# A two-layer gated decoder trunk: one ordering edge ahead of the values' block product, and the last 128 tokens sent in quarters

## The chip, the cores and the metric

The kernel runs on one core of a Trainium2 chip. The metric is the device time of one execution in microseconds (us), the median of several runs. The core has five engines, each with its own in-order queue of instructions: TensorE (PE in the profile; its weight loads are listed apart as PEld), VectorE (DVE), ScalarE (ACT), GpSimd (POOL) and SyncE (SP). In this kernel SP's queue issues most loads and stores, POOL's issues the accumulating DMAs, and ACT's queue issues a few stores. Tiles live in the on-chip memories SBUF and PSUM; matmuls write PSUM banks of 128 x 512 float32.

## What is computed

Two layers, each with sliding-window attention and a retention branch merged by sigmoid gates, and a squared-ReLU MLP; 512 tokens, model width 1024. Cut to what matters here:

```python
def hybrid_layer(x, g_mix, w_in, sinks, w_a, w_b, w_out, g_mlp, w_up, w_down):
    h = rmsnorm(x, g_mix)
    z = h @ w_in
    aq, ak, av, rq, rk, rv, rg, ga, gb = jnp.split(z, SPLIT_POINTS, axis=-1)
    ya = sliding_window_sink_attention(rope(aq), rope(ak), av, sinks) @ w_a
    r = chunkwise_retention(rotate(rq), rotate(rk), rv)
    r = r * lax.rsqrt(jnp.mean(r * r, axis=-1, keepdims=True) + EPS)
    r = r.reshape(B, S, RET_V) * jax.nn.silu(rg)
    yb = r @ w_b
    x = x + (jax.nn.sigmoid(ga) * ya + jax.nn.sigmoid(gb) * yb) @ w_out
    x = x + jnp.square(jax.nn.relu(rmsnorm(x, g_mlp) @ w_up)) @ w_down
    return x

def reference(x, ...):
    for l in range(2):
        x = hybrid_layer(x, ...)
    return rmsnorm(x, g_final)
```

The change touches two places: the projections `rg` (the retention's output gates, here their upper 512 columns) and `rv` (the retention's values), which both multiply the normalized input by columns of `w_in`, and the final RMSNorm with the store of the output.

## The kernel before

**Precision and weights.** All products are in float32r and split in two: each operand is written as a high part (`hi`) plus a low part (`lo`), and a product is three matmuls, hi by hi, hi by lo and lo by hi (lines 394, 395 and 396 in the helper `products`; `multiply` in `last_gates` does the same at its own line 1015). Weights come in units of 128 x 1024. A call of `unit()` (line 354) takes the next unit in a fixed order, and before that splits units ahead of it: the load into `raw` is issued on SP's queue, ACT copies `raw` into `hi` (line 342), and DVE subtracts to get `lo` (line 343). There are four buffers each of `hi` and `lo` (`SPLIT + 1`), so a split can start only when a unit that was used earlier has been read by its last matmul.

**Block products.** Several projections are computed by seven products of half-size blocks instead of eight, with sums and differences of blocks formed first. For the moving or stationary side these sums are built by the class `Turned` (`turned[1]` to `turned[4]`); the matching sums of weights are made in memory by accumulating DMAs of POOL and by DVE adds at line 322. Two functions that follow each other in the program use them:

- `last_gates(turned)` (lines 1004 to 1058) has seven products of 24 matmuls of 256 columns each, on three PSUM banks `a`, `b` and `c`. In the program's order they are: quarter (0,0) into `a`; a copy of `a` into `b`; `turned[1]` into `c`; `five = keep(c, -1)`, an ACT copy out of `c` (line 1026); `turned[2]` onto `b`; `sum_two = keep(b, 1)`; quarter (1,0) onto `a`; `put(0, 0)`; quarter (1,1) onto `c`; `put(0, 1)`; `turned[3]` onto `b`; `put(1, 1, b, -1, five)`, which begins with a DVE instruction that reads `b` (line 1033); `turned[4]` onto `b`; `put(1, 0)`. A product that adds onto a bank cannot start before the copy or `put` that reads the bank's earlier state. `done(i)` applies the SiLU (ACT sigmoid at 1062, DVE product at 1063).
- `values(turned)` (lines 925 to 984) has the same seven steps with two weight units each, on two banks at a time, matmuls of 512 columns. Its first product is `multiply(a, quarter(0, 0))` at line 967: 24 matmuls, which need only the normalized input `xh`, `xl` and the first two units of `rv`.

**What sets the order.** The program is written in one stream, and the framework's planner puts each engine's instructions into the order in which it expects them to become ready, program order deciding among ready ones. So instructions of `values` may come ahead of instructions of `last_gates` in TensorE's queue. `tc.issue_after(ins)` puts every instruction that its block traces on the engine of `ins` behind `ins` in that engine's queue. It orders the queue and adds no wait for the result; instructions of other engines in the block are not touched. `latest[0]` is a list cell in which helpers leave the last matmul that they traced.

**The end.** In the last layer the output of each block of 128 tokens is held as two halves of 512 columns: `v`, columns 512 to 1023, and `self.y[0, j, m]`, columns 0 to 511. `Ending.put` (lines 1713 to 1741) adds the last product to `v` (DVE, line 1711), takes the sum of squares (ACT, line 1727, with DVE at 1733), the square root (ACT, line 1735) and the reciprocal (DVE, line 1736). Then DVE scales `v` by that factor and the gain (line 1737) and SP's queue sends it (line 1738), while ACT scales the other half, which already has its gain (line 1740), and ACT's queue sends that (line 1741). The last block is (j, m) = (1, 1). `TOKENS` (line 999) is the pair of slices 0 to 255 and 256 to 511.

Of the kernel before, what the change touches and what calls it, by code (L numbers as in the profile page):

```python
# [12 lines left out]
AF = mybir.ActivationFunctionType  # L13
ALU = mybir.AluOpType
# [4 lines left out]
T = 512  # L19
# [97 lines left out]
def decoder(ctx, tc, xT, x_first, w_in, w_rg, w_rv, w_a, w_b, w_wo, w_up, w_pair, w_down, w_end, tables, decay, band, g_last, out):  # L117
    nc = tc.nc
# [279 lines left out]
    latest, behind, spread = [None], [], []  # L398
# [222 lines left out]
    def layer_body(layer):  # L621
# [299 lines left out]
        def quarter(half, tokens):  # L921
            at = slice(tokens * H, tokens * H + H)
            return [(xh[:, k, at], xl[:, k, at]) for k in range(4 * half, 4 * half + 4)]

        def values(turned):

            a, c = ([bank(ps_mm, "rv") for _ in range(2)] for _ in range(2))
            b = [bank(pool, "rv") for pool in (ps_mm, ps_aux)]
            nc.tensor.matmul(b[1], ones, xh[:, 0, :], start=True, stop=True)
            plus, minus = rms_mix.columns, small.tile([P, NB], F32, tag="ncol", name="ncol", bufs=1)  # L930
            nc.vector.tensor_scalar(minus, plus, -1.0, None, ALU.mult)

            def multiply(ps, moving, start=True):
                for u in range(2):
                    hi, lo = unit("rv", layer)
                    for m in range(2):
                        at = slice(m * P, (m + 1) * P)
                        pairs = []
                        for k in range(2):
                            xh_, xl_ = moving[2 * u + k]  # L940
                            cols = slice(k * T, (k + 1) * T)
                            pairs.append(((xh_[:, at], xl_[:, at]), (hi[:, cols], lo[:, cols])))
                        products(ps[m], pairs, start and u == 0, u == 1, not start)

            def scale(j, m, sign):
                return (plus if sign > 0 else minus)[:, 2 * j + m : 2 * j + m + 1]

            def keep(j, ps, sign):
                got = []
                for m in range(2):  # L950
                    t = temp("kept")
                    nc.scalar.activation(t, ps[m], AF.Copy, scale=scale(j, m, sign))
                    got.append(t)
                return got

            def put(i, j, ps, sign, kept=None):
                for m in range(2):
                    hi, lo = slots.one(), slots.one()
                    if kept:
                        nc.vector.scalar_tensor_tensor(kept[m], ps[m], scale(j, m, sign), kept[m], ALU.mult, ALU.add)  # L960
                        split(view(hi), view(lo), kept[m])
                    else:
                        split(view(hi), view(lo), ps[m], scale(j, m, sign))
                    rv[i, 2 * j + m] = (hi, lo)
                    pace(f32(view(hi)))

            multiply(a, quarter(0, 0))
            for m in range(2):
                nc.scalar.activation(b[m], a[m], AF.Copy)
            multiply(c, turned[1])  # L970
            five = keep(1, c, -1)
            multiply(b, turned[2], False)
            turned.free(0)
            two = keep(1, b, 1)
            multiply(a, quarter(1, 0), False)
            quiet[0] = False
            put(0, 0, a, 1)
            multiply(c, quarter(1, 1), False)
            put(0, 1, c, 1, two)
            multiply(b, turned[3], False)  # L980
            put(1, 1, b, -1, five)
            multiply(b, turned[4], False)
            turned.free(1)
            put(1, 0, b, -1)
# [14 lines left out]
        TOKENS = (slice(0, H), slice(H, T))  # L999
# [4 lines left out]
        def last_gates(turned):  # L1004

            a, b, c = (bank(ps_mm, "rg") for _ in range(3))
            two = [big("z") for _ in range(2)]

            def multiply(ps, moving, start=True):
                hi, lo = unit("rg", layer)  # L1010
                for k, (vh, vl) in enumerate(moving):
                    for n in range(2):
                        o, cols = ps[:, n * H : (n + 1) * H], slice((2 * k + n) * P, (2 * k + n + 1) * P)
                        for w, v in ((hi, vh), (hi, vl), (lo, vh)):
                            nc.tensor.matmul(  # L1015
                                o,
                                w[:, cols],
                                v,
                                start=start and k == 0 and n == 0 and w is hi and v is vh,
                                stop=k == 3 and n == 1 and w is lo,  # L1020
                                skip_group_check=True,
                            )

            def keep(ps, sign):
                t = temp("kept")
                nc.scalar.activation(t, ps, AF.Copy, scale=float(sign))
                return both(t)

            def put(i, j, ps, sign, kept=None):
                v = two[i][:, :, TOKENS[j]]  # L1030
                by = rstd()[:, TOKENS[j]].unsqueeze(1).broadcast_to([P, 2, H])
                if kept is not None:
                    nc.vector.scalar_tensor_tensor(kept, both(ps), float(sign), kept, ALU.mult, ALU.add)
                    nc.vector.tensor_tensor(v, kept, by, ALU.mult)
                else:
                    nc.vector.scalar_tensor_tensor(v, both(ps), float(sign), by, ALU.mult, ALU.mult)

            def done(i):
                for m in range(2):
                    rg[4 + 2 * i + m] = two[i][:, m, :]  # L1040
                    silu(4 + 2 * i + m)

            multiply(a, quarter(0, 0))
            nc.scalar.activation(b, a, AF.Copy)
            multiply(c, turned[1])
            five = keep(c, -1)
            multiply(b, turned[2], False)
            sum_two = keep(b, 1)
            multiply(a, quarter(1, 0), False)
            put(0, 0, a, 1)  # L1050
            multiply(c, quarter(1, 1), False)
            put(0, 1, c, 1, sum_two)
            done(0)
            multiply(b, turned[3], False)
            put(1, 1, b, -1, five)
            multiply(b, turned[4], False)
            put(1, 0, b, -1)
            done(1)
# [622 lines left out]
        class Ending:  # L1681
# [31 lines left out]
            def put(self, i, j, m, ps, sign, at=slice(0, T)):  # L1713
                block = 2 * j + m
                scale = (factor if sign > 0 else negative)[:, block : block + 1]
                if i and not last:
                    if (j, m) == (0, 1):
                        self.add(i, j, m, ps, scale)
                    else:
                        self.join(i, j, m, ps, scale)  # L1720
                    return
                with tc.issue_after(self.queued) if i else ExitStack():
                    self.add(i, j, m, ps, scale, at)
                if last:
                    v = self.y[i, j, m]
                    first, total, both = (sq[:, n * NB + block : n * NB + block + 1] for n in range(3))
                    nc.scalar.activation(temp("junk")[:, at], v[:, at], AF.Square, accum_out=both if i else first)
                    if not i:
                        nc.vector.tensor_tensor(v, v, last_gain[:, i, :], ALU.mult)
                        self.queued = nc.vector.tensor_scalar(first, first, 1.0 / D, EPS, ALU.mult, ALU.add).ins  # L1730
                        return
                    if at.stop < T:
                        nc.vector.scalar_tensor_tensor(first, both, 1.0 / D, first, ALU.mult, ALU.add)
                        return
                    nc.scalar.activation(total, both, AF.Sqrt, bias=first, scale=1.0 / D)
                    nc.vector.reciprocal(total, total)
                    nc.vector.scalar_tensor_tensor(v, v, total, last_gain[:, 1, :], ALU.mult, ALU.mult)
                    nc.sync.dma_start(out[:, block, T:], v)
                    v = self.y[0, j, m]
                    nc.scalar.activation(v, v, AF.Copy, scale=total)  # L1740
                    nc.scalar.dma_start(out[:, block, :T], v)

            def turn(self, i, j, half, pool):
                ps = bank(pool, "turn")
# [268 lines left out]
```

## Time and profile before

| | before |
|---|---|
| median of 3 runs | 1460.27 us (1459.97 to 1462.33) |
| profiled execution, its time | 1461.38 us |
| profiled execution, its span on the core | 1459.6 us |
| granted TensorE clock, mean over the span | 0.999 |
| instructions | 22457 |

The profile is of one execution. Its span runs from the first to the last instruction on the core. Most views list groups or single instructions as: start (us), duration (us), engine, line, operation, output<-inputs, shape; a number in square brackets is the time for which the engine stood idle just before, and what ended it. A view of waits lists who waited for whom, with the total in us, the number of times and the longest. In the views by stretches of time, each row has the stretch, its length, the busy time of PE, PEld, DVE, ACT and POOL with the number of instructions, the granted clock, the mean busy share of the 16 DMA engines and their GB/s. Matmuls are pipelined, so recorded durations overlap, and the distance from start to start is the pace.

### The profile page before, as it was taken

How to read it: one execution, taken by the hardware profiler on the slowest of the kernel's cores; microseconds unless marked ns; L12 is line 12 of the kernel's file. 1: busy time of each engine (PE TensorE's matmuls, PEld its weight loads, DVE VectorE, ACT ScalarE, POOL GpSimd, SP SyncE). 2: the span in 40 equal slices, each digit the busy share in tenths (PEclk: the TensorE clock that was granted, in tenths of full speed). 3: DMA queues.
4: the chain of work that ended last, by engine and by line, in shares of the span. 5: the costliest groups of instructions: out<-in, count | busy, mean ns of one | idle time of the engine just before them, and what ended most of it. 6: DMA issues, size and time to landing. Idle time of an engine off the chain costs nothing.

```text
span 1459.6 us, 22457 instructions
## 1 busy us (share of the span) xinstructions
PE 1447.5 (99%) x8185; PEld 1269.5 (87%) x8185; DVE 1183.1 (81%) x1776; ACT 976.5 (67%) x1593; POOL 222.1 (15%) x335
## 2 busy tenths in 40 slices
PE   9999999999999999999999999999999999999998
PEld 7888888888989999999888888888889899999997
DVE  6977987877898888888778789878688888888885
ACT  6656665543688777777756576655447887777775
POOL 0021002221101111112201110021210011111120
PEclk9999999999999999999999999999999999999999
DMA  7598349999735777666955974499965477777764
GB/s 259 178 292 221 118 134 302 286 275 283 212 115 200 196 190 194 174 178 182 305 174 185 287 201 155 147 314 283 274 185 170 144 196 201 196 189 200 177 188 143
DMA packets 97294, 302.83 MB, mean 207 GB/s; under 512 B 11424, under 2 KB 11552, under 8 KB 90784
## 3 DMA queue, kind: packets, MB, share of 16 engines
q0 software_dynamic: 36512, 129.78, 38.0%
q1 hardware_dynamic: 59952, 170.32, 33.9%
q8 instruction: 64, 1.05, 0.3%
q10 hardware_dynamic: 720, 1.31, 0.2%
q14 instruction: 46, 0.38, 0.1%
HBM read 261.78 MB, written 120.06 MB: 262 GB/s over the span
## 4 chain that ended last, share of the span: by engine, by line
PE 95%; DVE 2%; ACT 1%; issue 0%; DMA 0%; DVEq 0%
PE mm L394 22%; PE mm L396 22%; PE mm L395 22%; PE wo L1354 5%; PE b L394 3%; PE b L395 3%; PE b L396 3%; PE rg L1015 2%; PE rv L394 2%; PE rv L395 2%; PE rv L396 2%; PE mm L410 2%; PE score L780 1%; PE pT L745 1%; PE r L395 1%; PE r L396 1%
## 5 line engine op out<-in xcount | busy, mean ns | idle before, releaser
L342 ACT ACTIVATE hi<-raw 128x1024 fp32r<-128x1024 f32 (+1 forms) x393 | 400.1, 1022 | 264.6 <-PE mm L395 118.4
L343 DVE TENSOR_TENSOR lo<-raw,hi 128x1024 fp32r<-128x1024 f32 (+1 forms) x394 | 459.3, 1175 | 103.1 <-ACT hi L342 101.5
L395 PE MATMUL mm<-xl,hi 128*128 128x512 f32 (+1 forms) x912 | 319.4, 353 | 0.0
L394 PE MATMUL mm<-xh,hi 128*128 128x512 f32 (+1 forms) x912 | 318.5, 353 | 0.7 <-ACT xh L420 0.7
L396 PE MATMUL mm<-xh,lo 128*128 128x512 f32 (+1 forms) x912 | 315.6, 352 | 0.0
L394 PEld LDWEIGHTS mm<-xh,hi 128*128 128x128 f32 x912 | 173.1, 190 | 23.3 <-ACT xh L420 1.4
L395 PEld LDWEIGHTS mm<-xl,hi 128*128 128x128 f32 x912 | 173.3, 190 | 21.9
L396 PEld LDWEIGHTS mm<-xh,lo 128*128 128x128 f32 x912 | 171.9, 190 | 21.4
L395 PE MATMUL mm<-r,hi 128*128 128x256 f32 (+1 forms) x608 | 189.2, 311 | 0.0
L396 PE MATMUL mm<-r,lo 128*128 128x256 f32 (+1 forms) x608 | 189.0, 311 | 0.0
L394 PE MATMUL mm<-r,hi 128*128 128x256 f32 (+1 forms) x608 | 186.9, 311 | 0.5 <-ACT mm L1529 0.5
L394 PEld LDWEIGHTS mm<-r,hi 128*128 128x128 f32 x608 | 115.7, 190 | 9.1 <-ACT mm L1529 0.7
L395 PEld LDWEIGHTS mm<-r,hi 128*128 128x128 f32 x608 | 115.7, 190 | 8.5 <-DVE r L418 0.4
L396 PEld LDWEIGHTS mm<-r,lo 128*128 128x128 f32 x608 | 115.8, 190 | 6.3
L1679 POOL DMA_DIRECT2D y<-eu x56 | 63.2, 1407 | 368.0 <-DVE eu L1662 367.6
L395 PE MATMUL mm<-lo,r 128*128 128x512 f32 (+1 forms) x276 | 104.4, 388 | 0.0
L396 PE MATMUL mm<-hi,r 128*128 128x512 f32 (+1 forms) x276 | 101.2, 387 | 0.2 <-DVE r L418 0.2
L394 PE MATMUL mm<-hi,r 128*128 128x512 f32 (+1 forms) x276 | 98.2, 389 | 0.3 <-ACT r L417 0.2
L394 PE MATMUL b<-hi,r 128*128 128x512 f32 x180 | 70.5, 391 | 0.0
L395 PE MATMUL b<-lo,r 128*128 128x512 f32 x180 | 70.2, 390 | 0.0
L1354 PE MATMUL wo<-r,hi 128*128 128x256 f32 x384 | 69.3, 283 | 0.0
L283 DVE TENSOR_TENSOR raw<-raw 128x512 f32<-128x512 f32 x56 | 38.5, 688 | 36.0 <-DMA raw<-w_pair_in 31.1
(337 smaller groups left out, 2865.5 us busy)
## 6 DMA issues: line engine op xcount, KB each, us to landing
raw<-w_in_in SPq DMA_DIRECT2D x65, 512.0 KB, 5.6
sums_down<-w_down_in POOLq DMA_DIRECT2D x30, 1024.0 KB, 12.2
sums_up<-w_pair_in POOLq DMA_DIRECT2D x56, 512.0 KB, 11.1
raw<-w_down_in SPq DMA_DIRECT2D x45, 512.0 KB, 7.2
raw<-w_pair_in SPq DMA_DIRECT2D x84, 256.0 KB, 3.6
y<-y POOLq DMA_DIRECT2D x62, 256.0 KB, 9.7
y<-eu POOLq DMA_DIRECT2D x61, 256.0 KB, 8.6
raw<-sums_down SPq DMA_DIRECT2D x30, 512.0 KB, 7.6
```

The lines of the kernel that those rows point to most:

```text
L283: nc.vector.tensor_tensor(raws[i][:, at], last[:, LEFT], last[:, RIGHT], ALU.add)
L342: state["high"] = nc.scalar.activation(hi[:, at], raw[:, at], AF.Copy).ins
L343: nc.vector.tensor_tensor(lo[:, at], raw[:, at], f32(hi[:, at]), ALU.subtract)
L394: nc.tensor.matmul(ps, ah, bh, start=start and i == 0, stop=False, **more)
L395: nc.tensor.matmul(ps, ah, bl, start=False, stop=False, **more)
L396: latest[0] = nc.tensor.matmul(ps, al, bh, start=False, stop=stop and i == n - 1, **more).ins
L410: latest[0] = nc.tensor.matmul(ps, w[:, cols(j, c)], moving[k][low], start=first, stop=bool(final)).ins
L745: nc.tensor.transpose(pt[:, i * P : (i + 1) * P], sm[:, at : at + P], ident)
L780: nc.tensor.matmul(ps[:, g * w : (g + 1) * w], q_s[g][:, c, at], part[:, keys], start=i == 0, stop=i == 1)
L1015: nc.tensor.matmul(o, w[:, cols], v, start=start and k == 0 and n == 0 and w is hi and v is vh, stop=k == 3 and n == 1 and w is lo, skip_g ...
L1354: latest[0] = nc.tensor.matmul(o, w[:, cols], v, start=start and first and n % 2 == 0 and w is hi and v is vh, stop=final and w is lo, ski ...
L1679: nc.gpsimd.dma_start(y[:, 2 * j + m, i * T : (i + 1) * T], t, **how)
```

## The change

Two edits. In `values`, the first product is traced inside `issue_after(latest[0])`, and `last_gates` now leaves its matmuls in `latest[0]`; so each of the first product's 24 matmuls stands behind the last traced matmul of `last_gates` in TensorE's queue, in both layers. At the end, for the block (1, 1) alone, the two scalings and the two stores of 512 columns become four of 256 columns each; of the four stores SP's queue issues three and ACT's queue the last. For the other three blocks the same instructions remain.

```diff
@@ values
-            multiply(a, quarter(0, 0))
+            with tc.issue_after(latest[0]):
+                multiply(a, quarter(0, 0))
@@ last_gates, multiply
-                            nc.tensor.matmul(
+                            latest[0] = nc.tensor.matmul(
                                 o,
                                 w[:, cols],
                                 v,
...
                                 skip_group_check=True,
-                            )
+                            ).ins
@@ Ending.put
-                    nc.vector.scalar_tensor_tensor(v, v, total, last_gain[:, 1, :], ALU.mult, ALU.mult)
-                    nc.sync.dma_start(out[:, block, T:], v)
-                    v = self.y[0, j, m]
-                    nc.scalar.activation(v, v, AF.Copy, scale=total)
-                    nc.scalar.dma_start(out[:, block, :T], v)
+                    w = self.y[0, j, m]
+                    final = (j, m) == (1, 1)
+                    for n, p in enumerate(TOKENS if final else (slice(0, T),)):
+                        nc.vector.scalar_tensor_tensor(v[:, p], v[:, p], total, last_gain[:, 1, p], ALU.mult, ALU.mult)
+                        nc.sync.dma_start(out[:, block, T + p.start : T + p.stop], v[:, p])
+                        nc.scalar.activation(w[:, p], w[:, p], AF.Copy, scale=total)
+                        queue = nc.sync if final and n == 0 else nc.scalar
+                        queue.dma_start(out[:, block, p], w[:, p])
```

## The prediction

> **What bounds the kernel now.** I read the page's engine line first, then what TensorE itself waited for, then the order in which TensorE, ScalarE (ACT) and VectorE (DVE) ran the last gates' block, then the last five microseconds.
>
> ```profile
> PE 1447.5 (99%) x8185; PEld 1269.5 (87%) x8185; DVE 1183.1 (81%) x1776; ACT 976.5 (67%) x1593; POOL 222.1 (15%) x335
> ...
> PE 95%; DVE 2%; ACT 1%; issue 0%; DMA 0%; DVEq 0%
> ```
>
> TensorE is busy for 1447.5 of 1459.6 us and carries 95% of the chain that ended last. So time can be had in two places only: where TensorE stands still between its first and last matmul, and behind its last matmul. Everything else is covered by matmuls.
>
> ```profile
> PE rv L394 <- ACT hi L342: 2.1, 2, 1.0
> PE warm L374 <- DVE ones L369: 1.1, 1, 1.1
> PE mm L394 <- ACT xh L420: 0.7, 1, 0.7
> ```
>
> The longest entry of TensorE's waits is the one this change goes for: twice, once in each layer, a first matmul of the values' block (rv) waits 1.03 us for its high weights. The rest are small and elsewhere.
>
> **The place, as TensorE ran it in layer 0.**
>
> ```profile
> 184.28 0.28 PE L1015 MATMUL rg<-r,lo 128*128 128x256 f32 x1
> 185.59 0.73 PE L394 MATMUL rv<-hi,xh 128*128 128x512 f32 x2 [1.03 <-ACT hi L342]
> 186.16 0.30 PE L1015 MATMUL rg<-xh,hi 128*128 128x256 f32 x1
> ...
> 191.81 0.28 PE L1015 MATMUL rg<-r,lo 128*128 128x256 f32 x1
> 191.93 0.40 PE L395 MATMUL rv<-lo,xh 128*128 128x512 f32 x1
> 192.16 0.40 PE L396 MATMUL rv<-hi,xl 128*128 128x512 f32 x1
> ...
> 196.71 0.39 PE L396 MATMUL rv<-hi,xl 128*128 128x512 f32 x1
> 196.94 0.40 PE L1015 MATMUL rg<-r,hi 128*128 128x256 f32 x2
> ...
> 199.69 0.28 PE L1015 MATMUL rg<-r,lo 128*128 128x256 f32 x1
> 199.81 0.40 PE L394 MATMUL rv<-hi,r 128*128 128x512 f32 x1
> ```
>
> The gates' block has seven products of 24 matmuls. By 184.40 four are done (both that move `turned[1]` and `turned[2]`, and quarters (0,0) and (1,0)). The fifth, quarter (1,1) into bank `c`, starts at 186.16; the sixth, `turned[3]` into bank `b`, ends at 191.93; the seventh, `turned[4]`, again into `b`, runs from 196.94 to 199.81. The values' first product, also 24 matmuls, lies in two holes: 2 of it before the fifth product and 22 between sixth and seventh. Its pace is 0.23 us a matmul (191.93 to 192.16), that of the gates 0.12 (199.69 to 199.81).
>
> The question is what fills these holes once the values' product may not.
>
> ```profile
> 184.48 1.06 ACT L342 ACTIVATE hi<-raw 128x1024 fp32r<-128x1024 f32 x1 [0.26 <-PE rg L1015]
> 185.44 1.07 ACT L1026 ACTIVATE kept<-rg 128x512 f32<-128x512 f32 x2
> ```
> ```profile
> 186.07 0.19 PEld L1015 LDWEIGHTS rg<-xh,hi 128*128 128x128 f32 x1 [0.19 <-ACT kept L1026]
> ```
>
> The fifth product adds onto bank `c`, and `five = keep(c, -1)` must have read `c` first. ACT took the values' weight split first (184.48, when a weight buffer came free, just before the last of the four products ended at 184.28 + 0.28 = 184.56) and the two `keep` copies behind it, from 185.44. The first of the two ends near 186.02, and the weight load of the fifth product is recorded as waiting for just that, until 186.07. So the two rv matmuls did not hold the fifth product up; they used 0.45 us of a hole that ACT makes.
>
> ```profile
> 189.31 0.69 DVE L1033 SCALAR_TENSOR_TENSOR kept<-rg,kept 128x512 f32<-128x512 f32 x1 [2.05 <-PE rg L1015]
> 190.04 0.69 DVE L1034 TENSOR_TENSOR z<-kept,rstd 128x512 f32<-128x512 f32 x1
> 190.65 1.22 DVE L343 TENSOR_TENSOR lo<-raw,hi 128x1024 fp32r<-128x1024 f32 x1
> 191.79 0.68 DVE L1063 TENSOR_TENSOR z<-z,sig 128x512 f32<-128x512 f32 x1
> 192.39 0.68 DVE L1033 SCALAR_TENSOR_TENSOR kept<-rg,kept 128x512 f32<-128x512 f32 x1
> ```
>
> The seventh product adds onto `b` after the sixth, and `put(1, 1, b, -1, five)` (L1033, the second of these) must have read `b` in between: 192.39 to 193.07. Today 22 rv matmuls cover that wait.
>
> **The first edit, part by part.** It adds no instruction and removes none. It adds an ordering edge on TensorE alone, from each of the 24 matmuls to the last gates' matmul, in each layer. The weight splits (ACT, DVE) and loads (SP's queue) that the same block issues get no edge, since they are not TensorE's; I take their order from the trace as it is, because ACT's choice at 184.48 and DVE's chain from 189.31 hang on gates' matmuls that come before any moved one.
>
> First hole: today 184.28 + 0.12 = 184.40 to 186.16 is 1.76 us with 2 x 0.23 us of work, 1.31 lost (the matmuls' own rows). Afterwards the load still begins at 186.07 and the product at 186.16, with nothing in the hole: 1.67 to 1.76 lost. Second hole: today nothing lost. Afterwards L1033 ends at 193.07, a release takes about 0.05 (split ends 185.54, rv's matmul 185.59), and the matmul stands up to 0.09 behind its load (186.07 to 186.16): the seventh product starts at 193.12 to 193.21 where its slot was 191.93, so 1.19 to 1.28 lost. Together 2.86 to 3.04 against 1.31: 1.55 to 1.73 more per layer.
>
> The same places in layer 1:
>
> ```profile
> 907.04 0.28 PE L1015 MATMUL rg<-r,lo 128*128 128x256 f32 x1
> 908.35 0.73 PE L394 MATMUL rv<-hi,xh 128*128 128x512 f32 x2 [1.03 <-ACT hi L342]
> 908.92 0.30 PE L1015 MATMUL rg<-xh,hi 128*128 128x256 f32 x1
> ...
> 914.68 0.40 PE L395 MATMUL rv<-lo,xh 128*128 128x512 f32 x1
> ```
> ```profile
> 915.15 0.69 DVE L1033 SCALAR_TENSOR_TENSOR kept<-rg,kept 128x512 f32<-128x512 f32 x1
> ```
>
> 907.16 to 908.92 is again 1.76, and 915.84 + 0.05 to 0.14 against 914.68 is 1.21 to 1.30. Both layers: 3.1 to 3.5 us; I take 3.3, nearer the rows as they stand.
>
> The product itself then runs as one piece, 24 x 0.23 = 5.5 us, behind the seventh. I cost its move at nothing: its weights were split long before (184.48, and DVE's at 190.65), and what queues behind it (the values' next products) has weights split at or before it. It holds two of the four weight buffers until about 198.8 and 201.5 (seventh product from 193.2, 2.9 long, then 12 x 0.23 for each unit); the splits that wait for those buffers serve the product after the next, not before 201.5 + 5.5 = 207, and need 1.06 (ACT) and 1.22 (DVE). That slack is the cover; gone, each late split would show about 2.3. Nothing later gives the loss back: TensorE's other waits are 0.7 us and less and hang on its own results, so they move along. Nor does a hole of 1.8 us slow the matmuls behind it: in the end's rows below, the granted clock is still 1.00 in the slice to 1456.60, 3.4 us after TensorE let DVE go at 1453.14.
>
> **The second edit.** Today, the end:
>
> ```profile
> 1453.14 0.48 DVE L1711 SCALAR_TENSOR_TENSOR x<-mm,columns,x 128x256 f32<-128x256 f32 x1 [0.18 <-PE mm L396]
> ...
> 1454.80 0.72 ACT L1740 ACTIVATE x<-x,sq 128x512 f32<-128x512 f32 x1 [0.23 <-DVE sq L1736]
> 1454.80 0.75 DVE L1737 SCALAR_TENSOR_TENSOR x<-x,sq,late 128x512 f32<-128x512 f32 x1
> 1455.55 0.37 ACTq L1741 DMA_DIRECT2D y_out<-x  x1
> 1455.58 0.33 SPq L1738 DMA_DIRECT2D y_out<-x  x1
> ```
> ```profile
> 1456.40:1456.60 0.20, 0.00 (x0) 0.00 (x0) 0.00 (x0) 0.00 (x0) 0.00 (x0) 1.00 0.99 379
> ...
> 1457.60:1457.80 0.20, 0.00 (x0) 0.00 (x0) 0.00 (x0) 0.00 (x0) 0.00 (x0) 0.50 0.87 308
> 1457.80:1458.00 0.20, 0.00 (x0) 0.00 (x0) 0.00 (x0) 0.00 (x0) 0.00 (x0) 0.50 0.08 21
> ```
>
> Issue at 1455.55, first bytes at 1456.40 (0.85 later), then 1.4 us of a full stream. A 256-wide DVE instruction takes 0.48 for 0.75 at 512, so the first quarter is ready at 1455.28, 0.27 earlier. Two more DMAs are issued: SP sends at about 1455.30, 1455.64 and 1455.98 (0.33 each), ACT its one near 1455.73. The last first-byte is then due at 1456.83, when half the bytes are still to go, so the stream stays full and ends 0.27 earlier. Unknown is the rate of 1 KB rows. If each took as long as a 2 KB row the stream would double: 1.1 us lost. If size costs nothing: 0.27 won. Only 128 packets of the whole run have between 512 B and 2 KB, by the page; they are the mask's rows of 1 KB, and they ran between 12.05 and 13.5 us:
>
> ```profile
> DMA packets 97294, 302.83 MB, mean 207 GB/s; under 512 B 11424, under 2 KB 11552, under 8 KB 90784
> ```
> ```profile
> DMA packets 320, 0.58 MB, mean 400 GB/s; under 512 B 37, under 2 KB 165, under 8 KB 320
> ```
>
> 400 GB/s with 128 such packets (165 less 37) of 320 in that stretch, where the end's 2 KB rows make 379: nearly no loss. I take 0.25 won.
>
> From issue to landing the list of DMA issues of the last 20 us (median, us) has:
>
> ```profile
> y_out<-x SPq DMA_DIRECT2D x4, 256.0 KB, 2.4
> ```
>
> The Trainium skill ("DMA: Bandwidth & Descriptors", section on the anatomy of one DMA) puts about 2.0 us plus bytes/436e3 on each DMA, so by it the last quarter, issued at 1455.98, would land after 2.3 us, at 1458.28, against 1455.58 + 2.6 = 1458.18 today, and the sum would be 0.35 higher. The trace has 2.4 us for these 256 KB, 0.2 less than the page.
>
> **Sum.** Span 1459.6 + 3.3 - 0.25 = 1462.65. The profiled execution took 1461.38 with 1459.6 of span; the median shown is 1460.27, so the forecast for the median is 1460.27 + 3.05 = **1463.3 us**, own range 1462.9 to 1463.7.
>
> **Rivals.**
> (1) The block runs through: the `keep` and L1033 are arranged so that neither hole stays. For it: both are short, and the 1.03 us wait is what the profile blames. Against: the load at 186.07 waits for `kept`, and no other ready work is recorded between 191.93 and 196.94. Price: 2 x 1.31 + 0.25 won, 1457.4; not slower. It decides if fifth and seventh products start within 0.2 us of their predecessors.
> (2) ACT takes `five` before the values' split: `c` is complete at 184.56, `five` ends 185.2, the fifth product starts near 185.25, 0.91 earlier per layer: 1463.3 - 1.8 = 1461.5. Against: the split was ready first.
> (3) DVE puts one more 1.14 us split ahead of the second L1033, or a split misses its use: 1463.3 + 2.3 = 1465.6. For: DVE is busy without a break from 189.31.
> (4) The order does not change and only the end does: 1460.0. Against: the edge names these very matmuls.
>
> **How the numbers follow.** Forecast 0.66; rivals 0.06, 0.13, 0.09, 0.06. About 0.2% (2.9 us) is what a measurement here can tell from no change, and the forecast lies just above it: of its 0.66 I count 0.43 as slower and 0.23 as within. With (3), slower 0.52; with (2) and (4), within 0.42; faster 0.06, from (1). The range leaves out (1), (3) and half of (4): 1460.0 to 1464.4.
>
> **What would show it.** Right: no rv matmul among L1015's, fifth product still behind `kept`, a new wait of the seventh product's L1015 for DVE L1033 near 1.2 us in both layers, first bytes of the end 0.27 earlier. Wrong: fifth product starting by 185.3, or anything but L1033 ahead of the seventh.

## The result and the profile after

| | before | after |
|---|---|---|
| median, 7 runs each | 1460.27 us (1459.34 to 1462.73) | 1464.68 us (1463.54 to 1467.05) |
| ratio after/before | | 1.0030, 95% interval 1.0019 to 1.0042 |
| span of the profiled execution | 1459.6 us | 1465.3 us (time 1467.05) |
| instructions | 22457 | 22467 |

The change costs 4.4 us. The forecast was 1463.3 with a range to 1464.4: the direction is right, and the median lies 0.28 us beyond the range. In the changed file lines stand one further down in the gates' and values' blocks (1015 is now 1016, 1026 is 1027, 1033 is 1034); the end's scalings are at 1741 and 1743, their stores at 1742 and 1745.

The first three entries of TensorE's waits after the change (who waited for whom, total us, times, longest):

```profile
PE rg L1016 <- ACT kept L1027: 3.0, 2, 1.5
PE rg L1016 <- DVE kept L1034: 2.1, 2, 1.0
PE warm L374 <- DVE ones L369: 1.1, 1, 1.1
```

The old first entry (rv for its `hi`) is gone, and two of the gates' own waits have come in its place, each once per layer. TensorE in layer 0, then in layer 1:

```profile
184.83 0.28 PE L1016 MATMUL rg<-r,lo 128*128 128x256 f32 x1
186.62 0.39 PE L1016 MATMUL rg<-xh,hi 128*128 128x256 f32 x1 [1.52 <-ACT kept L1027]
...
192.35 0.28 PE L1016 MATMUL rg<-r,lo 128*128 128x256 f32 x1
193.68 0.50 PE L1016 MATMUL rg<-r,hi 128*128 128x256 f32 x2 [1.04 <-DVE kept L1034]
...
196.53 0.28 PE L1016 MATMUL rg<-r,lo 128*128 128x256 f32 x1
196.66 0.40 PE L394 MATMUL rv<-hi,xh 128*128 128x512 f32 x1
...
909.58 0.28 PE L1016 MATMUL rg<-r,lo 128*128 128x256 f32 x1
911.38 0.39 PE L1016 MATMUL rg<-xh,hi 128*128 128x256 f32 x1 [1.52 <-ACT kept L1027]
...
917.11 0.28 PE L1016 MATMUL rg<-r,lo 128*128 128x256 f32 x1
918.43 0.50 PE L1016 MATMUL rg<-r,hi 128*128 128x256 f32 x2 [1.04 <-DVE kept L1034]
```

A gates' matmul has a pace of 0.12, so the first hole, layer 0's, is 186.62 - (184.83 + 0.12) = 1.67 us and the second 193.68 - (192.35 + 0.12) = 1.21; layer 1 has 1.68 and 1.20. Before, 1.31 of the first was lost and nothing of the second: 1.57 more per layer. No rv matmul stands among the gates' any more; the first one follows the last gates' matmul at once.

What ACT and DVE ran at these places is what they ran before, in the same order (shifted by 0.55 us):

```profile
185.03 1.06 ACT L342 ACTIVATE hi<-raw 128x1024 fp32r<-128x1024 f32 x1 [0.26 <-PE rg L1016]
185.99 1.07 ACT L1027 ACTIVATE kept<-rg 128x512 f32<-128x512 f32 x2
```
```profile
192.34 0.69 DVE L1064 TENSOR_TENSOR z<-z,sig 128x512 f32<-128x512 f32 x1
192.94 0.69 DVE L1034 SCALAR_TENSOR_TENSOR kept<-rg,kept 128x512 f32<-128x512 f32 x1
```

The end, in order of time, and then the stores' stream (the last two columns are the share of the DMA engines and GB/s):

```profile
1460.19 0.91 ACT L1743 ACTIVATE x<-x,sq 128x256 f32<-128x256 f32 x2 [0.23 <-DVE sq L1737]
1460.19 0.88 DVE L1741 SCALAR_TENSOR_TENSOR x<-x,sq,late 128x256 f32<-128x256 f32 x2
1460.71 0.33 SPq L1742 DMA_DIRECT2D y_out<-x  x1
1461.13 0.37 ACTq L1745 DMA_DIRECT2D y_out<-x  x1
1461.14 0.37 SPq L1745 DMA_DIRECT2D y_out<-x  x1
1461.61 0.45 SPq L1742 DMA_DIRECT2D y_out<-x  x1
```
```profile
1461.50:1461.70 0.20, 0.00 (x0) 0.00 (x0) 0.00 (x0) 0.00 (x0) 0.00 (x0) 0.50 0.67 236
1461.70:1461.90 0.20, 0.00 (x0) 0.00 (x0) 0.00 (x0) 0.00 (x0) 0.00 (x0) 0.50 1.06 338
1461.90:1462.10 0.20, 0.00 (x0) 0.00 (x0) 0.00 (x0) 0.00 (x0) 0.00 (x0) 0.50 0.59 185
1462.10:1462.30 0.20, 0.00 (x0) 0.00 (x0) 0.00 (x0) 0.00 (x0) 0.00 (x0) 0.50 1.00 348
...
1463.10:1463.30 0.20, 0.00 (x0) 0.00 (x0) 0.00 (x0) 0.00 (x0) 0.00 (x0) 0.50 0.51 164
```

Counted from the scalings' start, the first bytes come 0.27 us earlier than before (1461.53 - 1460.19 = 1.34 against 1456.41 - 1454.80 = 1.61, by the packets in the trace). But the stream then has a dip (185 GB/s) and in its full slices runs at 333 to 348 GB/s, where those of the 2 KB rows had 348 to 410, about 380 on average. From first to last byte it takes 1.78 us against 1.51, so its last bytes come 3.1 us behind the scalings' start in both kernels. The span's end comes 5.1 us behind it, against 4.8 before. So the end lost about 0.3 us instead of winning 0.25, and it lost them **behind the last byte**. There SP passes the program's last waits, among them one instruction for each of the eight semaphores that count the transfers of SP's and ACT's queues, before the core may finish. These are SP's instructions from the moment on at which the last store had landed, before and after; the first of each group is the wait that this landing ended:

```profile
L2008 SPq EVENT_SEMAPHORE  x2: 28/28/28, 1458.4 to 1458.4; - x2
```
```profile
L2012 SPq EVENT_SEMAPHORE  x7: 27/28/28, 1463.7 to 1464.1; - x7
```

Two before, seven after, about 0.06 us apart. The semaphore numbers that the trace keeps with each instruction show why: transfers by SP's and ACT's queues are counted by eight semaphores in turn (numbers 100, 102, 104 and 106 to 110, here called 0 to 7), and the last waits ask for them in the order 0 to 7. Before, the last two stores were counted by 6 and 7, the end of that list. Two transfers more move the last four stores to 6, 7, 0 and 1, so the store that lands last is asked for early, and six waits for what has long landed are still to be passed.

### The profile page after: what moved, and what is told of

It reads as the page before. It is cut to its first block, busy times and chain, and to the rows that moved or that the text cites. A ratio compares the mean times of both kernels' runs of the same rounds, so it can differ in the third digit from the quotient of the medians.

```text
span 1465.3 us, 22467 instructions
## 1 busy us (share of the span) xinstructions
PE 1449.1 (99%) x8185; PEld 1270.3 (87%) x8185; DVE 1183.5 (81%) x1777; ACT 976.2 (67%) x1594; POOL 228.0 (16%) x335
```

## The experiments

Each ratio is to runs of the kernel before on the same chip, with its 95% interval. The expectations count a hole from the start of the matmul ahead of it plus 0.23 us, where the sections above and below take 0.12; what they call 1.57 and 1.10 is 1.67 and 1.21 here. Diffs are cut to the lines that matter; `...` marks what is left out.

**The change once more, its two parts alone, and another filling of the first hole.** The change's file unchanged:

> The changed kernel as it is, a second look. Theory: of the 4.4 us, 3.5 are the two new waits of the gates' block (about 1.57 for ACT's kept and 1.1 for DVE's L1034, in each layer, less the 1.2 that before loses there) and 0.3 the end; they must be there again, and the ratio should be near 1.0026 (3.8 us). Rival: the further loss behind 1180 us in the first profile (0.45 + 0.39 us on a weight add whose load landed late) belongs to the change and is there again, and the ratio is 1.003 or more.

1464.05 us against 1460.89, ratio 1.0026 (1.0017 to 1.0035). In its trace the holes are the same to 0.01 us, and the end takes 5.1 us from the scalings' start.

The first edit alone (`edge_only`) and the second alone (`quarters_only`):

```diff
@@ edge_only: values and last_gates as in the change, Ending.put as before
@@ quarters_only: Ending.put as in the change, values and last_gates as before
```

> The first edit alone, the end as before. Theory: +3.5 us (1.0024), with the waits of the gates' block as in the changed kernel and 4.8 us from the reciprocal's last start to the end of the span. Rival (the end is the larger part): below +2 us.

> The second edit alone. Theory: +0.3 us (the 1 KB rows stream at 335 instead of 380 GB/s and the completion comes later, which gives back the 0.25 us by which the first bytes start earlier): span from the last scaling's start to the end 5.1 against 4.8 us; the ratio can't be told from 1. Rival (the prediction's pricing): 0.25 us less than before, 4.55.

The edge alone: 1464.49 against 1460.89, 1.0024 (1.0014 to 1.0034), both holes as in the change, the end 4.8 us. The quarters alone: 1462.19, 1.0008 (0.9999 to 1.0017), the end 5.1 us. The edge carries nearly all of it; the quarters win nothing and probably lose a little. The interval of the quarters alone reaches no change, so that they lose is read from the trace of the end.

`c_first` leaves both edits away and changes the order ahead of the hole: the second half of the third product must wait for the second product, so that bank `c` is done 12 matmuls earlier.

```diff
-            def multiply(ps, moving, start=True):
+            def multiply(ps, moving, start=True, behind=None):
...
+                            with tc.issue_after(behind) if behind is not None and k > 1 else ExitStack():
+                                done_last[0] = nc.tensor.matmul(
...
-            multiply(b, turned[2], False)
+            multiply(b, turned[2], False, done_last[0])
```

> Before, with one other edge: in the gates' block the second half of the turned[2] product stands behind the turned[1] product, so that bank c is complete 1.4 us earlier and its ACT copy runs beside matmuls. No edge on the values' product. Theory (the first hole is ACT's copy out of c, not the values' matmuls at its end): the hole of 1.2 us goes, the fifth product follows at once, and each layer is 0.7 to 1.2 us shorter: -1.4 to -2.4 us, ratio 0.9985 to 0.999. Rival (the hole is set by the weight split of the values): the hole stays and nothing changes.

1460.02 us, 0.9995 (0.9986 to 1.0003), which can't be told from no change. Of the hole 0.24 us is left in layer 0 (183.48 to 183.72), and no wait of a gates' matmul for ACT's `kept` is listed any more. TensorE's waits show where 1.2 us of the gain went:

```profile
PE rg L1018 <- DVE r L418: 1.2, 2, 0.8
```

The second product, taken earlier, now waits for the split of its own operand `r` on DVE, 0.4 us in layer 0 and 0.8 in layer 1.

**The two holes apart, and who makes the first.** In `edge_fifth` the values' first product waits for the fifth gates' product only.

```diff
-            multiply(a, quarter(0, 0))
+            with tc.issue_after(state["fifth"]):
+                multiply(a, quarter(0, 0))
...
```

> Before, with only the end as it was and the values' first product kept behind the fifth gates' product instead of the seventh; it may fill the second hole as before. If the two holes are independent prices: the first hole loses 1.57 instead of 1.31 us per layer, the second stays filled (no wait of the seventh product for DVE's sum), so +0.5 us in all, ratio 1.0003 to 1.0005. If a hole kept filled gives nothing back, because the values' product then ends at another time and what follows it waits: as the whole edge, 1.0024.

1462.53 against 1461.43, 1.0008 (0.9999 to 1.0016). In the trace the first hole is 1.67 us in both layers, and no wait of a gates' matmul for DVE is listed: the second hole is filled again, by rv matmuls. By its holes it costs 2 x (1.67 - 1.31) = 0.7 us, which the interval holds; the whole edge's 1.0024 lies outside it. The holes are separate prices.

In `edge_five` the edge stays, and ACT takes `five` ahead of the values' weight split.

```diff
-                    state["high"] = nc.scalar.activation(hi[:, at], raw[:, at], AF.Copy).ins
+                    with tc.issue_after(state.pop("five")) if name == "rv" and "five" in state else ExitStack():
+                        state["high"] = nc.scalar.activation(hi[:, at], raw[:, at], AF.Copy).ins
...
```

> The edge of the change with the end as before, and ACT takes the first of the two `kept` copies (five) ahead of the values' weight split. Theory: the first hole is made by that split of 1.06 us; it shrinks from 1.57 to between 0.65 and 0.85 us per layer, the second stays at 1.10; 1.5 to 1.8 us less than the edge alone, ratio 1.0012 to 1.0014. Rival: the later split makes DVE's part of it later and with it the second sum, the second hole grows by as much, and the ratio stays at 1.0024.

TensorE in layer 0:

```profile
184.24 0.28 PE L1017 MATMUL rg<-r,lo 128*128 128x256 f32 x1
185.21 0.38 PE L1017 MATMUL rg<-xh,hi 128*128 128x256 f32 x1 [0.69 <-ACT kept L1028]
...
190.93 0.28 PE L1017 MATMUL rg<-r,lo 128*128 128x256 f32 x1
192.19 0.51 PE L1017 MATMUL rg<-r,hi 128*128 128x256 f32 x2 [0.97 <-DVE kept L1037]
```

The first hole is 185.21 - (184.24 + 0.12) = 0.85 instead of 1.67, the second 1.14 instead of 1.21: 0.9 us less per layer. The time is 1462.43 against 1461.43, 1.0009 (1.0000 to 1.0018), where the edge alone had 1.0024. So ACT's order, split first, makes half of the first hole, and the later split harms nothing.

`c3_five` leaves the edge away again and puts both cures together: 6 matmuls held back instead of 12 (`k > 2` in `c_first`'s edit), and `edge_five`'s edit.

> Before without the edge, with two orders changed ahead of the hole: the last 6 matmuls of the third product (turned[2]) are held behind the second's (turned[1]), and ACT takes five ahead of the values' weight split. Theory: of the 1.31 us lost per layer, 0.7 is covered by the 6 matmuls and 0.8 goes with the split, so at most 0.3 is left, 2.0 to 2.6 us less than before, ratio 0.9982 to 0.9987. Rival: as with 12 matmuls held back, part goes into waits for the split of r on DVE, 0.4 us or more per layer, ratio 0.999 and up.

1461.15 against 1461.43, 1.0000 (0.9991 to 1.0009): a miss. ACT shows the reason:

```profile
181.97 1.06 ACT L343 ACTIVATE hi<-raw 128x1024 fp32r<-128x1024 f32 x1 [1.10 <-PE rg L1019]
182.94 0.58 ACT L1030 ACTIVATE kept<-rg 128x512 f32<-128x512 f32 x1
183.41 1.05 ACT L343 ACTIVATE hi<-raw 128x1024 fp32r<-128x1024 f32 x1
```

The values' split does stand behind `five` now, but with `c` done earlier the split before it, of the seventh gates' product's weights, falls just ahead of `five`. TensorE's hole was 183.57 - (182.50 + 0.12) = 0.95 us. `c3_five2` puts `five` ahead of that split too (the edge holds from the second split behind `five` in the program on):

```diff
+                    five, first = state.get("five", (None, len(order)))
+                    with tc.issue_after(five) if i >= first else ExitStack():
...
+                    state["five"] = kept, state["split"] + 1
...
```

> As the kernel before this in the same line (6 matmuls of turned[2] held back, five ahead of the values' weight split), with five also ahead of the weight split one before it, the seventh gates' product's. Theory: in the run before, the hole of 0.85 us per layer was made by that other split, which ACT ran while five was ready; now at most 0.15 us per layer is left of the 1.31, 2.3 to 2.6 us less than before, ratio 0.9982 to 0.9985. Rival: the seventh product's weights come late instead, or the time goes into another wait as with 12 matmuls held back; then 0.999 and up.

ACT, and TensorE at the same place:

```profile
182.02 0.60 ACT L1033 ACTIVATE kept<-rg 128x512 f32<-128x512 f32 x1 [1.22 <-PE rg L1022]
182.51 2.00 ACT L344 ACTIVATE hi<-raw 128x1024 fp32r<-128x1024 f32 x2
```
```profile
182.42 0.28 PE L1022 MATMUL rg<-r,lo 128*128 128x256 f32 x1
182.67 0.39 PE L1022 MATMUL rg<-xh,hi 128*128 128x256 f32 x1
```

The hole is 182.67 - (182.42 + 0.12) = 0.13 us, and no wait of a gates' matmul is left among TensorE's listed waits. The time is 1458.05 us against 1460.68, **0.9984 (0.9975 to 0.9993)**: faster than the kernel before and than the change. The rv matmuls keep the second hole filled, as before the change.

**The end.** Three other forms of the last stores, one profile each:

```diff
@@ tail_rows: before, last block only
+    nc.sync.dma_start(out[:, block, T:].rearrange("p (a t) -> p a t", a=2), v.rearrange("p (a t) -> p a t", a=2))
...
@@ tail_parts: before, last block only, two by SP and two by ACT
+    for q in (slice(0, 64), slice(64, P)):
+        nc.sync.dma_start(out[q, block, T:], v[q])
+        nc.scalar.dma_start(out[q, block, :T], w[q])
@@ tail_22: before, with the change's end but
-    queue = nc.sync if final and n == 0 else nc.scalar
-    queue.dma_start(out[:, block, p], w[:, p])
+    nc.scalar.dma_start(out[:, block, p], w[:, p])
```

> Before, with the last store's two transfers described as 1 KB rows (two per partition) instead of 2 KB; still two transfers, whole scalings. If the row size sets the rate: about 338 GB/s in place of 380, the stream 0.15 to 0.25 us longer, end 4.95 to 5.05 us after the scalings' start. If the number of transfers and their issue set it: 380 GB/s and 4.8 us.

The end came at 4.8 us, but this tested nothing. The packets of that stretch in `tail_rows`, then in the change:

```profile
DMA packets 288, 0.52 MB, mean 262 GB/s; under 512 B 32, under 2 KB 32, under 8 KB 288
```
```profile
DMA packets 576, 0.52 MB, mean 250 GB/s; under 512 B 64, under 2 KB 576, under 8 KB 576
```

The 256 data packets stayed at 2 KB; the change has 512 of 1 KB. So no run sends the end in 1 KB rows without four transfers, and whether the row size or the number of transfers lowers the rate stays open.

> Before, with the last store in four transfers of 64 partitions with 2 KB rows, two by each queue, behind whole scalings. If the row size set the loss: 380 GB/s and an end 4.8 us after the scalings' start, as with two transfers. If the number of transfers set it: 340 GB/s or a later end, 5.0 us and up.

Neither: the end came 6.3 us behind the scalings' start. With 64 partitions a transfer, the stream had half the rate at a full share for its first 1.2 us:

```profile
1457.80:1458.00 0.20, 0.00 (x0) 0.00 (x0) 0.00 (x0) 0.00 (x0) 0.00 (x0) 0.50 1.04 225
...
1459.20:1459.40 0.20, 0.00 (x0) 0.00 (x0) 0.00 (x0) 0.00 (x0) 0.00 (x0) 0.50 1.11 389
```

> The change, but the quarters sent two by SP and two by ACT instead of three and one. If SP's three issues in a row set the end: the last bytes come 0.2 to 0.4 us earlier than with the change, end 4.7 to 4.9 us after the scalings' start. If the rate of 1 KB rows sets it: 335 to 340 GB/s and 5.0 to 5.1 us, as with the change.

The end came at 5.0 us and the stream had 317 to 358 GB/s without a dip, its last bytes 3.0 us behind the scalings' start instead of 3.1: SP's three issues in a row go with the dip, but they are not what sets the end. The last two stores, too, are counted by semaphores 0 and 1, and SP passed seven waits behind the last landing. That raised the theory of the order of waits, which two kernels test. They load decay tables in more pieces, far from the end (`rot_before` one table per layer, two transfers more in all; `rot_quarters` both, six more); the order of all compute engines' instructions is as in `before` and in `quarters_only`, and only the semaphores of the last stores move.

```diff
+            cuts = (0, T // 2, T) if pair == 0 else (0, T)                        # rot_before
+            cuts = (0, T // 4, T // 2, T) if pair == 0 else (0, T // 2, T)        # rot_quarters, with the change's end
-            nc.sync.dma_start(decays[pair], decay[:, 2 * pair : 2 * pair + 2, :])
+            for c0, c1 in zip(cuts, cuts[1:]):
+                nc.sync.dma_start(decays[pair][:, :, c0:c1], decay[:, 2 * pair : 2 * pair + 2, c0:c1])
```

> Before with its end as it was; one decay table per layer is loaded in two pieces, so two transfers more, about a thousand us ahead of the end, and the last two stores are counted by the first two of the eight transfer semaphores instead of the last two. SP's waits behind its last store go through those eight in a fixed order. Theory: the late end of the change is that order: the last store's wait is now followed by 6 waits of 0.06 us instead of 1 or none, and the end comes 5.10 to 5.20 us after the scalings' start instead of 4.81, with the same two transfers of 2 KB rows. Rival: the quarters themselves are what ends late; then 4.8 here.

> Before with the change's end in quarters, and six transfers more in the decay tables' loads, so that the four last stores are counted by the last four of the eight transfer semaphores. Theory (order of SP's last waits): the last store's wait is again the last or last but one, and the end comes 4.70 to 4.80 us after the scalings' start instead of 5.06 to 5.09. Rival (1 KB rows and SP's issues in a row): 5.0 to 5.1 as with the change.

SP's waits behind the last landing, and the scalings' start, in `rot_before` and then in `rot_quarters`:

```profile
L2010 SPq EVENT_SEMAPHORE  x8: 28/28/28, 1459.1 to 1459.5; - x8
...
1455.55 0.75 DVE L1739 SCALAR_TENSOR_TENSOR x<-x,sq,late 128x512 f32<-128x512 f32 x1
```
```profile
L2013 SPq EVENT_SEMAPHORE  x1: 28/28/28, 1458.9 to 1458.9; - x1
...
1455.36 0.88 DVE L1742 SCALAR_TENSOR_TENSOR x<-x,sq,late 128x256 f32<-128x256 f32 x2
```

`rot_before` ends at 1460.7, 5.2 us behind the scalings' start, with the two 2 KB stores of before and without a quarter: the order of waits alone is enough for an end as late as the change's. `rot_quarters` needs a single wait, and SP is through the list 1459.0 - 1455.36 = 3.6 us behind the scalings' start, against 3.7 before and 4.0 in the change. Its span ends at 4.9, not at the 4.7 to 4.8 expected, because the steps of all engines that close the program took 1.3 us behind SP's list here, and 1.1 in the others; one profile doesn't say why.

## Why the prediction was right in direction and short in size

**The bound and the first edit: right.** The fifth product stands behind `kept`, with the load and matmul where the prediction put them: 1.67 us, forecast 1.67 to 1.76. The seventh product's new wait for DVE's second L1033 (now 1034) makes a hole of 1.21 and 1.20 us, forecast 1.19 to 1.28 in layer 0 and 1.21 to 1.30 in layer 1. Per layer the holes are 1.57 longer, forecast 1.55 to 1.73. From the fourth product's last matmul to the values' second product TensorE takes 17.17 us in each layer instead of 15.41: 1.76 more, 3.5 for both, and `edge_only` measures 3.6. So the term of 3.3 was 0.2 too small: the first matmuls behind a hole take about 0.1 us longer than their pace (186.62 to 186.85 is 0.23 instead of 0.12), which the sum left out. `edge_fifth` and `edge_five` show the two holes and their causes one by one.

**The product's move costed at nothing: right.** None of TensorE's waits after the change is for a split that came late behind the moved product, so rival (3) did not occur; `edge_five`, which makes one split later still, bears that cover out.

**The rivals.** (1) fell at once: both holes are there. (2) was wrong for the change, where the split still goes first, but its price was right: `edge_five` forces that order and the fifth product starts 0.82 us earlier per layer, where 0.91 was put down. (4) fell with the order in the trace.

**The second edit: the step that failed.** The prediction said that "the stream stays full and ends 0.27 earlier" and took 0.25 won; measured are about 0.3 lost. Its first part held, the first bytes being 0.27 us earlier. Three things were wrong. The rate of 2 KB rows was carried over: the quarters ran at 333 to 348 GB/s in full slices against about 380. The mask's window, from which the price was taken, holds loads and only 128 such packets. SP's issues were put 0.34 us apart and came 0.43 and 0.47 apart (1460.71, 1461.14, 1461.61), and the stream has a dip behind the first store; the two together eat the 0.27 us (in `tail_22`, which has no dip, the stream lasts 1.68). And the sum ended with the last byte; what SP does behind it was not looked at, though the view of SP's instructions in the trace of before has it. By the end of SP's list the second edit is worth at most 0.1 us won (3.6 us in `rot_quarters`, one profile, against 3.7 before); the order of SP's last waits turned this into about 0.3 lost.

The section of the Trainium skill that the prediction cites ("DMA: Bandwidth & Descriptors", anatomy of one DMA) states its fit, 2.3 us for 128 KB, for DMAs on GpSimd's path; these stores were issued by SP and ACT. The list of DMA issues after the change has 2.1:

```profile
y_out<-x SPq DMA_DIRECT2D x3, 128.0 KB, 2.1
```

So it was luck that the sum by this fit was nearer to the time: the stores did not land later, the last of them 3.5 us behind the scalings' start against 3.6 before.

**The range.** With both terms as measured the sum is 1460.27 + 3.5 + 0.3 = 1464.1, inside the range and at the 1.0026 of the repeat. The remaining 0.6 us of the first measurement lie within its interval. The range was made by which rivals it leaves out and had no room for this scatter, whose size the three runs of before (1459.97 to 1462.33) already showed. The profiled execution after, itself the slowest of its runs, shows two parts of it: 0.55 us are lost within the first 11 us, and a weight load that comes late in layer 1 costs about 1.1. DVE at that load, before and after:

```profile
1179.38 0.69 DVE L283 TENSOR_TENSOR raw<-raw 128x512 f32<-128x512 f32 x1 [2.65 <-DMA raw<-w_pair_in]
```
```profile
1184.74 0.69 DVE L283 TENSOR_TENSOR raw<-raw 128x512 f32<-128x512 f32 x1 [3.72 <-DMA raw<-w_pair_in]
```

It is 5.4 us later where TensorE was 4.3 behind. `edge_only` has the same delay, and `after_again`, the very kernel of the change, has next to none (0.1 us). `tail_rows`, where the engines' order is that of before, waits 3.50 us for this load and loses 0.8 us of TensorE's time at it. So the delay doesn't belong to the change. Why the load lands late in some runs stays open.

## What to carry to other kernels

Work that the planner puts into the middle of another block may be there because that block has a hole, as here; before it is moved out, look up what the gap it leaves waits for, and price the gap, not the wait that disappears. If such a wait is to be removed, its maker has to be moved: here the engine that frees the PSUM bank ran a weight split first, and ordering the copy ahead of two splits, with six matmuls held back, won about 2.3 us (ratio 0.9984), while the edge on TensorE lost 3.5 (1.0024). A term at the very end has to be followed to the last instruction of the core, not to the last byte: in this kernel any transfer that SP's or ACT's queue issues more can change which semaphore counts the last store, and with it the end.

## What was not expected of the hardware

- SP needs about 0.06 us for a wait whose semaphore is long there, so their order behind the last landing is worth up to 0.4 us (5.2 against 4.8 us behind the scalings' start, with the same stores).
- Stores of the same bytes in 128 rows a transfer ran at about 380 GB/s as two transfers of 2 KB rows and at about 340 as four of 1 KB rows (which of the two matters is not separated); as 64 rows of 2 KB a transfer they ran at 174 to 225 while two queues were at it, with the DMA engines' share near 1.
- TensorE's first matmuls go at half their pace (0.43 us instead of 0.23 for 512 columns) while the granted clock is recorded as 1.00, and where this ends differs from run to run: at 4.2 us in the profile of `c3_five2`, at 6.7 in that of `after_again` and at 10.4 in that of the change, the same kernel as `after_again`. At 11 us, ahead of any instruction that the edits touch, the first and the last of these are 2.4 us apart. The Trainium skill ("TensorE: Matmul & The Clock Gate", Part 1 on the clock gate) describes a warm-up at half the clock and says that it varies by run. Its 3.4 us from the first matmul (here at 1.06) agree with the profile of `c3_five2`, not with the other two. The slice from 8 to 9 us has 4 matmuls in the change's profile and 6 in that of `c3_five2`, with the clock in the third column from the right:

```profile
8.00:9.00 1.00, 1.00 (x4) 0.81 (x3) 1.00 (x3) 1.00 (x3) 0.00 (x0) 1.00 1.02 391
```
```profile
8.00:9.00 1.00, 1.00 (x6) 0.84 (x5) 1.00 (x3) 1.00 (x3) 0.00 (x0) 1.00 1.08 367
```
